# Splitting a 768-column product into 384 + 384 instead of 512 + 256

## Chip, cores and metric

The kernel runs on one core of one Trainium2 chip. The metric is device time in microseconds. The kernel before takes 2879.85 us, the median of three runs (2879.68 to 2881.93).

## What is computed

The reference is two layers of a diffusion backbone on 512 latent tokens and 256 context tokens of width 1024, in float32. Each layer is a SwiGLU feed-forward block, a token mixing block and a second feed-forward block, all of them modulated:

```
h   = modulate(rms_norm(x), shift, scale)
x  += 0.5 * gate * (silu(h @ w_gate) * (h @ w_up)) @ w_down        # width 2816
h   = modulate(rms_norm(x), shift, scale)
x  += gate * concat(attention(GQA), short_conv, attention(MLA)) @ w_out   # all from h @ w_in
x  += second half-step feed-forward, as the first
```

Latent and context tokens share all weights. Only the latent stream is returned, so the context stream ends after the attention of the second layer: three of the four feed-forward blocks work on all 768 tokens, the last one on the 512 latent tokens.

## The kernel before, in words

All activations are held transposed: the model dimension on the partitions (eight tiles of 128), tokens along the columns, latent tokens in columns 0 to 511 and context tokens in columns 512 to 767 of tiles that are 768 wide. A float32 product is made of three products of rounded parts: each operand is split into a high part and a remainder, and `mm3` (line 192) issues high times high, high times low and low times high. For each of the three it walks over `segs(cols)` (line 183), which cuts a column range at column 512: a product over all 768 tokens is thus one matmul of 512 columns and one of 256. Both read the same stationary weights, and each matmul instruction comes with a weight load of its own in the trace.

```
for st, mv, f, l in ((wh, rh, first, False), (wh, rl, False, False), (wl, rh, False, last)):
    for s in segs(cols):
        te.matmul(out=pt[:, s], lhsT=st, rhs=mv[:, s], start=f, stop=l)
```

`project` (line 197) calls `mm3` for every 128-row tile of the contraction: eight tiles, or seven or eight in the down projection. The result lies in a PSUM tile made by `ps()` (line 98), 1024 columns of float32, which are two banks of 512; there are two such tiles. Columns 0 to 511 of the product fill the first bank and columns 512 to 767 half of the second. Four more single banks come from `po()`.

In a feed-forward block (`ffn`, line 422) the 22 tiles of the inner width are done in three chunks of 8, 7 and 7. For each tile a gate and an up product are made into the two `ps` tiles; ScalarE takes silu out of the gate product, VectorE multiplies it with the up product, and the result is split again. The first two of the 22 tiles are done with latent and context columns apart, because their latent products are started while the norm ahead of them is still running. After each chunk `residual` (line 302) makes the down projection: eight output tiles over all columns, except that the last chunk of a block does only five in this way and the last three with latent and context columns apart. `update` (line 311) adds each product, times a per-row gate, to `xT`, in one VectorE instruction for the latent columns and one for the context columns.

Products over all 768 tokens are also made in `mixing` (line 625): the second convolution group (`conv`, line 645) in the first layer, the compressed keys (`ckv`) in both layers and the compressed queries (`cq`) in the first, with `evac` (line 779) and `Stats.square` (line 229) reading them, and five output tiles of the output projection of the first layer.

Weights come by DMA on the SP queue (`wload`, line 167, two buffers). ScalarE rounds them to the high part, VectorE subtracts to get the low part (`wsplit`, line 172, three buffers each). VectorE also computes the modulation vectors beside the feed-forward blocks (`mod_block`, line 128). Within a stretch marked by `chain(...)` and `unchain(...)` an engine keeps program order; elsewhere the framework's scheduler orders the instructions.

Of the kernel before, what the change touches and what calls it, by code (L numbers as in the profile page):

```python
# [15 lines left out]
P = 128  # L16
# [9 lines left out]
DEPTH = 2  # L26
EPS = 1e-6
LAT = slice(0, SEQ)
CTXS = slice(SEQ, T)
# [12 lines left out]
def tile_net(ctx: ExitStack, tc: tile.TileContext, a, out):  # L42
# [7 lines left out]
    class Engine:  # L50
        """An engine whose instructions keep the program order inside a chain and stay behind it."""

# [58 lines left out]

    # ---------------------------------------------------------------- constants
    ident = const.tile([P, P], F32, name="ident")
# [8 lines left out]

    # ---------------------------------------------------------------- modulation
    mod = {}
# [40 lines left out]

    # ---------------------------------------------------------------- weights
    def wload(src, w):
# [15 lines left out]
    def segs(cols):  # L183
# [6 lines left out]
        return r  # L190

    def mm3(pt, wh, wl, rh, rl, cols, first, last):
        for st, mv, f, l in ((wh, rh, first, False), (wh, rl, False, False), (wl, rh, False, last)):
            for s in segs(cols):
                te.matmul(out=pt[:, s], lhsT=st, rhs=mv[:, s], start=f, stop=l)

# [6 lines left out]

    # ---------------------------------------------------------------- rsqrt and norms
    def rsqrt_steps(ms, n, tag="rs", bufs=3):
        """1/sqrt(ms) of a [P, n] tile, and the steps that compute it."""
        hm, y, t = (small(n, tag=tag + c, bufs=bufs) for c in "abc")
        steps = [lambda: ve.tensor_scalar_mul(hm, ms, -0.5),
                 lambda: ve.tensor_scalar(out=y.bitcast(I32), in0=ms.bitcast(I32), scalar1=-0.5, scalar2=1597463007.0,
                                          op0=ALU.mult, op1=ALU.add)]  # L210
        for _ in range(3):
            steps += [lambda: ve.tensor_mul(t, y, y), lambda: ve.tensor_mul(t, t, hm),
                      lambda: ve.scalar_tensor_tensor(out=y, in0=t, scalar=1.5, in1=y, op0=ALU.add, op1=ALU.mult)]
        return y, steps
# [7 lines left out]
    class Stats:  # L222
        """sum over the model dim of x^2, one stream."""

# [3 lines left out]

        def square(self, x):
            self.sq = slot() if self.acc is None else temp()  # L230
            se.activation(out=self.sq[:, :self.w], in_=x[:, self.cols], func=AF.Square)

# [6 lines left out]

        def add(self, x):  # L240
            self.square(x)
            self.accumulate()
# [34 lines left out]
    class HMod:  # L277
        """hi and lo of (x*A)*R + B for one model tile and one stream"""

# [22 lines left out]
    def residual(blocks, rhs, gate, streams, nxt, pre=None, late={}):  # L302
        """x += gate * (W^T rhs) for streams of (columns, modulation row); nxt = (layer, mod index) of the norm that
        follows, or None. pre: weight sources of the first products after that norm. Returns h and (weights, products)."""
        g = mod[gate]
# [10 lines left out]
        for o in range(KD - ntail):  # L316
            pt = ps()
            project(pt, blocks(o), rhs, full)
            for n, (cols, i) in enumerate(streams):
                update(o, pt[:, cols], cols, i)  # L320
                if two:
                    S[n].add(xT[o])
# [13 lines left out]

        # the norm of the first stream runs beside the last products of the second
        s1 = []
# [81 lines left out]

    # ---------------------------------------------------------------- FFN
    def ffn(l, f, hin, streams, nxt, pre, npump, late={}):
# [7 lines left out]
        for ci, (m0, nm_) in enumerate(CHUNKS):  # L430
            acts = []
            for m in range(m0, m0 + nm_):
                wgu = [E[2 * m + j] if 2 * m + j < len(E) else wblock(a[("wg", "wu")[j]][i, m]) for j in range(2)]
                if 2 * m < len(E):
# [6 lines left out]
                    for j in range(2):  # L441
                        project(pts[j], wgu[j], h, c1)
                    parts = ((first[0][:, c0], first[1][:, c0], c0), (pts[0][:, c1], pts[1][:, c1], c1))
                else:
                    pts = [ps(), ps()]
                    for j in range(2):
                        project(pts[j], wgu[j], h, cols)
                    parts = ((pts[0][:, :w], pts[1][:, :w], cols),)
                sg = temp()
                for g, u, c in parts:  # L450
                    se.activation(out=sg[:, c], in_=g, func=AF.Silu)
                    ve.tensor_mul(sg[:, c], u, sg[:, c])
                ah, al = slot(F32R), slot(F32R)
# [18 lines left out]

    # ---------------------------------------------------------------- attention
    side = []

    def trickle(n=2):
        """small DVE steps of side work between the large ones"""
        for _ in range(n):
            if side:
                side.pop(0)()  # L480

    class Unit:
        """two query blocks of one head"""

# [27 lines left out]
        def transposes(self, g):  # L512
            """key tiles 2g, 2g+1 of P^T"""
            if g >= self.ng:
# [56 lines left out]
    def attend(units, jobs):  # L571
        """units as a pipeline, every engine in the order given here; jobs[n, place] holds the other work of step n."""
        chain("te")
# [45 lines left out]

    # ---------------------------------------------------------------- token mixing  # L620
    def wn_block(l, k, c0, w, eng=None):
# [3 lines left out]
    def mixing(l, hin, early, streams, nxt, pre):  # L625
# [4 lines left out]
        nqt = wq // P  # L630
        # per-layer vectors
        gq = cst("gqk", l, [P, 512])
# [9 lines left out]

        # ---- conv
        mix = [None] * 8
        def conv(c):
# [3 lines left out]
            def product(j):  # L649
                if c:  # L650
                    pt = ps()
                    project(pt, wbs[j], h, qcols)
                    return [pt[:, qcols]]
                r = [accs[j][:, LAT]]
# [7 lines left out]
            for src, cols in zip(product(0), parts):  # L662
                se.copy(u[:, cols], src)
            for src, cols in zip(product(1), parts):
                ve.tensor_mul(u[:, cols], src, u[:, cols])
            y = slot()
# [6 lines left out]
            for src, cols in zip(product(2), parts):  # L673
                ve.tensor_mul(y[:, cols], src, y[:, cols])
            mix[3 + c] = y

        # ---- q, k, kr, v token-major
        qk = [None] * NT
# [36 lines left out]

        # ---- q, k norm and rope (token-major)
        ms = pool.tile([P, NT, 9], F32, name=nm("st2"), tag="st2", bufs=1)
# [4 lines left out]
        def rope_a(y, sin, nh, dh, t2f, e1):  # L722
            """swap(y)*sin over a [P, nh, dh] view"""
            b = dh // 4
# [8 lines left out]
        def rope_b(y, t2, cos, nh, e0):  # L733
            """y = y*cos + t2"""
            e0.tensor_mul(y, y, bc(cos, 1, nh))
# [9 lines left out]
        def twice(t):  # L745
            """both key heads twice, for a transpose into both halves of the partitions"""
            x = qk[t]
# [20 lines left out]

        # ---- transposed projections: ckv, cq
        comp = {"ckv": [], "cq": []}  # L770
# [8 lines left out]
        def evac(pt, name, g, w):  # L779
            ch, cl = slot(F32R), slot(F32R)  # L780
            se.mul(ch[:, :w], pt[:, :w], g)
            ve.scalar_tensor_tensor(out=cl[:, :w], in0=pt[:, :w], scalar=g, in1=f32(ch)[:, :w], op0=ALU.mult, op1=ALU.subtract)
            comp[name].append((ch, cl))

        for i in range(5):
# [17 lines left out]
            if i < 4:  # L803
                evac(pt, name, g, w)
                stats[name].add(pt)

        # ---- transposed keys and queries of the GQA heads
        def colsT(c, n, t0, alloc):
# [37 lines left out]
        query_split(q0, 0)  # L846
        stats["cq"].square(pt)
        key_split(k1, slot(F32R), pool.tile([P, T], F32R, name=nm("k2"), tag="mscr", bufs=1))
        query_split(q0, 1)
        stats["cq"].accumulate()  # L850

        # ---- MLA up-projections (token-major)
        st3 = pool.tile([P, NT, 18], F32, name=nm("st3"), tag="st3", bufs=1)
# [32 lines left out]
        def heads_of(t):  # L886
            """views [P, heads, 96] of the keys of token tile t, with their heads; the last tile lies in spare columns"""
            if t == packed:
# [35 lines left out]

        # ---- MLA norms (token-major), as side work
        def factors(ts, c, parts, r, tag):
            """rsqrt(mean((r*x)^2) + eps) * r for the sums of squares in the columns c of st3"""
            n, w = ts.stop - ts.start, c.stop - c.start
# [48 lines left out]

        # ---- attention
        lat_units = ((0, 1), (2, 3))
# [34 lines left out]
        def mla_part(hd, which, t0):  # L1014
            """queries (0) or keys (1) of one head transposed, from token tile t0 on; split when complete"""
            tok, n, w = ((query_of, nqt, wq), (key_of, NT, T))[which]
# [99 lines left out]

        # ---- output projection
        mix_split(7)
# [6 lines left out]

    # ---------------------------------------------------------------- the network
    chain("te", "ve", "se")
# [257 lines left out]
```

## Time and profile before

| | |
|---|---|
| median of three runs | 2879.85 us (2879.68 to 2881.93) |
| span of the profiled execution | 2882.5 us |
| mean granted TensorE clock | 0.993 |
| TensorE (PE) busy | 2782.3 us, 97% of the span, 15824 matmuls |
| VectorE (DVE) busy | 1496.3 us, 52% |
| ScalarE (ACT) busy | 898.4 us, 31% |
| GpSimd (POOL) busy | 189.9 us, 7% |

All rows come from one profiled execution; its span is the time from its first to its last instruction, and no time is recorded for what lies outside it. Its span is 2.65 us above the median of the runs. PE is the matrix engine; PEld are its weight loads, which overlap the matmuls. Matmuls are pipelined: the duration of one contains its latency, so neighbouring matmuls overlap, and what a matmul costs in a dense stretch is the distance from its start to the start of the next (its pitch), which is a stretch's length over its count.

### The profile page before, as it was taken

The page shows a single profiled execution, that of the slowest core. Times are in us where ns is not written, and L with a number is a line of the kernel's source. Part 1 is how long each engine was busy: PE and PEld are TensorE (multiplying, and loading weights), DVE is VectorE, ACT ScalarE, POOL GpSimd, SP SyncE. Part 2 cuts the span into 40 slices and gives each one's busy share as a digit, 9 for nine tenths or more (in the row PEclk, how much of TensorE's full clock was granted, in tenths as well). Part 3 has the DMA queues.
Part 4 walks back from the last instruction along what each step waited for, and adds up shares of the span by engine and source line. Part 5 has one row for each costly group of instructions (what it writes and reads, how often), then busy time and mean ns, then how long its engine had stood idle before and what let it go on. Part 6 is the DMA issues. An engine that isn't in the chain of part 4 may idle for free.

```text
span 2882.5 us, 38311 instructions
## 1 busy us (share of the span) xinstructions
PE 2782.3 (97%) x15824; PEld 2407.2 (84%) x15824; DVE 1496.3 (52%) x2498; ACT 898.4 (31%) x1451; POOL 189.9 (7%) x225
## 2 busy tenths in 40 slices
PE   7999999999988999999999999999999989999999
PEld 4888888889778888888888888888887788888887
DVE  6763645263788667546343642222235798633333
ACT  4211212232467632112122321221223478422221
POOL 0000000011232210000000100000001233100000
PEclk9999999999999999999999999999999999999999
DMA  6542533212100125434232342212122100233332
GB/s 216 162 153 75 157 112 110 60 47 72 35 1 9 52 75 168 130 100 153 92 110 70 112 148 66 62 57 72 57 61 61 61 8 16 74 103 95 90 101 88
DMA packets 79167, 251.51 MB, mean 87 GB/s; under 512 B 10896, under 2 KB 16528, under 8 KB 78992
## 3 DMA queue, kind: packets, MB, share of 16 engines
q1 hardware_dynamic: 78992, 249.06, 27.7%
q8 instruction: 124, 2.03, 0.3%
q14 instruction: 51, 0.42, 0.0%
HBM read 246.93 MB, written 2.10 MB: 86 GB/s over the span
## 4 chain that ended last, share of the span: by engine, by line
PE 84%; DVE 8%; ACT 5%; issue 2%; DMA 1%; POOL 0%; SPq 0%; DVEq 0%; ACTq 0%; POOLq 0%
PE ps L60 74%; PE po L60 10%; DVE m L60 3%; DVE s L60 3%; ACT t L60 2%; ACT s L60 1%; ACT ph L60 1%; DVE t L60 1%; DMA wr<-in_wiN_dram 0%; DVE wl L60 0%; ACT wh L60 0%; ACT ot L60 0%; DVE kr L60 0%; DMA xT<-in_xT_dram 0%; DVE pl L60 0%
## 5 line engine op out<-in xcount | busy, mean ns | idle before, releaser
L60 PE MATMUL ps<-s,wh 128*128 128x512 f32 (+1 forms) x7794 | 1782.0, 342 | 4.1 <-ACT wh L60 3.8
L60 PEld LDWEIGHTS ps<-s,wh 128*128 128x128 f32 x7794 | 1233.8, 188 | 197.5 <-ACT wh L60 4.5
L60 PE MATMUL ps<-s,wl 128*128 128x512 f32 (+1 forms) x3897 | 1086.9, 343 | 0.8 <-DVE wl L60 0.8
L60 ACT CAST wh<-wr 128x1024 fp32r<-128x1024 f32 (+1 forms) x308 | 314.8, 1024 | 1486.9 <-PE ps L60 984.6
L60 PEld LDWEIGHTS ps<-s,wl 128*128 128x128 f32 x3897 | 624.4, 188 | 96.4 <-DVE wl L60 1.9
L60 DVE TENSOR_TENSOR wl<-wr,wh 128x1024 fp32r<-128x1024 f32 (+3 forms) x298 | 354.2, 1190 | 269.1 <-ACT wh L60 267.0
L60 DVE SCALAR_TENSOR_TENSOR xT<-ps,mod,xT 128x256 f32<-128x256 f32 (+1 forms) x209 | 110.6, 566 | 407.7 <-PE ps L60 407.7
L60 DVE SCALAR_TENSOR_TENSOR mscr<-mr,sb 128x1024 f32<-128x1024 f32 x224 | 273.8, 1222 | 61.3 <-DMA mr<-in_wm_dram 57.8
L60 DVE TENSOR_TENSOR t<-ps,t 128x768 f32<-128x768 f32 (+2 forms) x91 | 76.7, 843 | 423.9 <-PE ps L60 422.9
L60 PE MATMUL po<-s,s 128*128 128x256 f32 (+2 forms) x856 | 133.9, 312 | 10.0 <-DVE s L60 3.1
L60 PE MATMUL po<-s,wh 128*128 128x512 f32 (+1 forms) x478 | 139.2, 375 | 0.7 <-ACT s L60 0.4
L60 PEld LDWEIGHTS po<-s,s 128*128 128x128 f32 x856 | 124.9, 194 | 14.4 <-DVE s L60 4.0
L238 POOL TENSOR_TENSOR s<-s,t 128x256 f32<-128x256 f32 x15 | 13.1, 876 | 1822.0 <-ACT t L60 1820.4
L60 DVE TENSOR_REDUCE m<-ps 128x1 f32<-128x768 f32 (+2 forms) x126 | 103.5, 821 | 27.7 <-PE ps L60 27.2
L60 PE MATMUL po<-ident,t 128*128 128x128 f32 x684 | 101.0, 279 | 15.0 <-ACT t L60 14.0
L60 ACT ACTIVATE t<-ps,m 128x768 f32<-128x768 f32 (+1 forms) x120 | 99.0, 825 | 23.0 <-DVE m L60 22.3
L60 PEld LDWEIGHTS po<-s,wh 128*128 128x128 f32 x478 | 86.4, 190 | 18.7 <-issue 0.9
L60 PEld LDWEIGHTS po<-ident,t 128*128 128x128 f32 x684 | 79.7, 143 | 19.7 <-ACT t L60 18.2
L60 PE MATMUL po<-s,wl 128*128 128x512 f32 (+1 forms) x239 | 90.1, 377 | 1.5 <-POOL wl L177 1.5
L60 ACT ACTIVATE t<-ps 128x768 f32<-128x768 f32 (+4 forms) x116 | 80.3, 692 | 18.1 <-DVE s L60 18.1
L60 DVE TENSOR_TENSOR s<-po,s 128x256 fp32r<-128x256 f32 (+5 forms) x139 | 71.5, 541 | 14.5 <-ACT s L60 12.2
L60 DVE TENSOR_TENSOR s<-t,s 128x768 fp32r<-128x768 f32 (+1 forms) x88 | 77.7, 883 | 0.9 <-ACT s L60 0.9
(147 smaller groups left out, 1964.5 us busy)
## 6 DMA issues: line engine op xcount, KB each, us to landing
mr<-in_wm_dram SPq DMA_DIRECT2D x128, 512.0 KB, 3.6
wr<-in_wg_dram SPq DMA_DIRECT2D x88, 512.0 KB, 3.5
wr<-in_wu_dram SPq DMA_DIRECT2D x88, 512.0 KB, 3.5
wr<-in_wd_dram SPq DMA_DIRECT2D x64, 448.0 KB, 3.4
wr<-in_wd_dram SPq DMA_DIRECT2D x32, 512.0 KB, 3.6
wr<-in_wiT_dram SPq DMA_DIRECT2D x22, 512.0 KB, 3.5
wr<-in_wo_dram SPq DMA_DIRECT2D x14, 512.0 KB, 3.5
s<-in_wm_dram SPq DMA_DIRECT2D x16, 384.0 KB, 6.5
```

Source lines behind the costliest of these rows:

```text
L60: f(*args, **kw)
L238: (eng or ve).tensor_add(self.acc[:, :self.w], self.acc[:, :self.w], sq[:, :self.w])
```

## The change

A product over all 768 columns is cut at column 384 instead of column 512. The first 384 columns go to columns 0 to 383 of the `ps` tile (first bank), the other 384 to columns 512 to 895 (second bank). Everything that reads such a product reads two pieces of 384 columns a bank apart, and writes them to 768 neighbouring columns. Products over the latent or the context columns alone are left as they are. Docstrings and comments are removed too.

```diff
+HALF = T // 2
+BANK = 512
...
+    def halves_of(cols):
+        if cols.start == 0 and cols.stop == T:
+            return [(slice(0, HALF), slice(0, HALF)), (slice(HALF, T), slice(BANK, BANK + HALF))]
+        return [(s, s) for s in segs(cols)]
+    def banks(pt):
+        return pt.rearrange("p (a b) -> p a b", b=BANK)[:, :, 0:HALF]
+    def pairs(t):
+        return t[:, 0:T].rearrange("p (a b) -> p a b", b=HALF)
...
+    def of_ps(pt, cols):
+        return banks(pt) if whole(cols) else pt[:, cols]
+    def of_sb(t, cols):
+        return pairs(t) if whole(cols) else t[:, cols]
     def mm3(pt, wh, wl, rh, rl, cols, first, last):
         for st, mv, f, l in ((wh, rh, first, False), (wh, rl, False, False), (wl, rh, False, last)):
-            for s in segs(cols):
-                te.matmul(out=pt[:, s], lhsT=st, rhs=mv[:, s], start=f, stop=l)
+            for s, d in halves_of(cols):
+                te.matmul(out=pt[:, d], lhsT=st, rhs=mv[:, s], start=f, stop=l)
...
             for n, (cols, i) in enumerate(streams):
-                update(o, pt[:, cols], cols, i)
+                if full.stop < T:
+                    update(o, pt[:, cols], cols, i)
+                else:
+                    for s, d in halves_of(full):
+                        lo, hi = max(s.start, cols.start), min(s.stop, cols.stop)
+                        if lo < hi:
+                            update(o, pt[:, d.start + lo - s.start:d.start + hi - s.start], slice(lo, hi), i)
...
-                    parts = ((pts[0][:, :w], pts[1][:, :w], cols),)
+                    parts = ((of_ps(pts[0], cols), of_ps(pts[1], cols), lambda t: of_sb(t, cols)),)
                 sg = temp()
-                for g, u, c in parts:
-                    se.activation(out=sg[:, c], in_=g, func=AF.Silu)
-                    ve.tensor_mul(sg[:, c], u, sg[:, c])
+                for g, u, of in parts:
+                    se.activation(out=of(sg), in_=g, func=AF.Silu)
+                    ve.tensor_mul(of(sg), u, of(sg))
```

In `residual` the latent columns 0 to 511 now lie in both banks, so `update` is called three times for an output tile instead of two: for 384 and 128 latent columns and for 256 context columns. `conv`, `evac` and `Stats.square` get the same two-piece views.

## Rows read from the trace of the kernel before

**Rows 1.** The profile page, its first part: busy time, share of the span and instructions of each engine.
```profile
PE 2782.3 (97%) x15824; PEld 2407.2 (84%) x15824; DVE 1496.3 (52%) x2498; ACT 898.4 (31%) x1451; POOL 189.9 (7%) x225
```

**Rows 2.** The span in stretches: from and to (us), length, then busy time and instructions of PE, PEld, DVE, ACT and POOL, the granted clock, the DMA share and GB/s. The second, sixth and eighth stretch below lie inside the three feed-forward blocks on 768 columns, the last one in the block on 512.
```profile
0.00:77.00 77.00, 58.34 (x285) 36.42 (x286) 47.81 (x109) 34.74 (x61) 0.70 (x6) 0.96 0.60 202
77.00:589.00 512.00, 512.00 (x2948) 448.31 (x2949) 267.89 (x390) 104.67 (x120) 0.00 (x0) 1.00 0.38 119
589.00:720.00 131.00, 125.16 (x739) 112.08 (x738) 65.64 (x134) 36.96 (x71) 18.01 (x14) 1.00 0.19 58
720.00:974.00 254.00, 221.53 (x1519) 201.58 (x1518) 204.34 (x403) 174.55 (x379) 72.00 (x92) 0.98 0.05 17
974.00:1077.00 103.00, 99.70 (x554) 85.20 (x553) 60.82 (x109) 33.91 (x52) 7.60 (x5) 1.00 0.23 72
1077.00:1580.00 503.00, 503.00 (x2887) 439.37 (x2887) 247.10 (x361) 100.42 (x113) 0.00 (x0) 1.00 0.38 118
1580.00:1637.00 57.00, 53.30 (x287) 44.64 (x286) 42.30 (x82) 20.60 (x33) 7.58 (x5) 1.00 0.23 74
1637.00:2141.00 504.00, 504.00 (x2897) 440.46 (x2896) 156.26 (x193) 100.35 (x113) 0.00 (x0) 1.00 0.27 82
...
2525.00:2882.00 357.00, 352.37 (x1532) 284.11 (x1530) 122.21 (x154) 86.75 (x105) 0.00 (x0) 1.00 0.31 95
```

**Rows 3.** Groups of PE's matmuls, shapes kept apart: names, contraction by stationary columns, moving shape, count, busy us, mean ns of one, idle us ahead of them. A matmul into `ps` from `s` (activations) and `wh` or `wl` (weights) is one of `project`'s.
```profile
L60 PE MATMUL ps<-s,wh 128*128 128x512 f32 x4258 | 1514.9, 394 | 3.8 <-ACT wh L60 3.8
L60 PE MATMUL ps<-s,wh 128*128 128x256 f32 x3536 | 946.8, 280 | 0.3 <-ACT sb L60 0.3
L60 PE MATMUL ps<-s,wl 128*128 128x512 f32 x2129 | 840.8, 395 | 0.8 <-DVE wl L60 0.8
L60 PE MATMUL ps<-s,wl 128*128 128x256 f32 x1768 | 494.6, 280 | 0.0
```

**Rows 4.** Pieces of the chain of work that ended last: start us, length us (start of the piece to start of the next), what, and how many instructions. The first two lie in the output projection of the first layer (768 columns as 512 + 256 alternating, then 512 alone), the last two in that of the second (512 alone, then 256 alone). `ps` is written in both of its banks only in the first.
```profile
974.32 42.00 PE ps L60 x240
1016.32 16.80 PE po L60 x72
...
2450.92 28.00 PE ps L60 x120
2478.92 8.64 PE po L60 x72
```

**Rows 5.** The timeline of PE in the product of queries by token tile (moving operand 384 columns wide, the weights `wn` at columns 0 and 384 of one 768-column tile): start us, us to the end of the last, what, how many; and then the first matmuls of a 384-column product after 256-column ones.
```profile
653.80 17.15 PE L60 MATMUL po<-s,s 128*128 128x384 f32 x98
...
862.16 0.34 PE L60 MATMUL ps<-wh,s 128*128 128x384 f32 x1
862.34 0.34 PE L60 MATMUL ps<-wl,s 128*128 128x384 f32 x1
862.52 0.51 PE L60 MATMUL ps<-wh,s 128*128 128x384 f32 x2
862.87 0.34 PE L60 MATMUL ps<-wl,s 128*128 128x384 f32 x1
863.04 0.51 PE L60 MATMUL ps<-wh,s 128*128 128x384 f32 x2
```

**Rows 6.** Groups of VectorE's instructions, shapes kept apart: the updates of `xT` out of a `ps` tile; columns as in rows 3.
```profile
L60 DVE SCALAR_TENSOR_TENSOR xT<-ps,mod,xT 128x256 f32<-128x256 f32 x141 | 65.0, 478 | 92.0 <-PE ps L60 92.0
L60 DVE SCALAR_TENSOR_TENSOR xT<-ps,mod,xT 128x512 f32<-128x512 f32 x68 | 51.0, 751 | 315.7 <-PE ps L60 315.7
```

**Rows 7.** The timeline of VectorE in the down projection of the first feed-forward block: start us, us, what, and in brackets its idle time ahead of it and who ended that.
```profile
241.37 1.14 DVE L60 SCALAR_TENSOR_TENSOR xT<-ps,mod,xT 128x512 f32<-128x512 f32 x2 [6.12 <-PE ps L60]
242.43 1.22 DVE L60 TENSOR_TENSOR wl<-wr,wh 128x1024 fp32r<-128x1024 f32 x1
249.77 1.14 DVE L60 SCALAR_TENSOR_TENSOR xT<-ps,mod,xT 128x512 f32<-128x512 f32 x2 [6.12 <-PE ps L60]
```

**Rows 8.** Groups of ScalarE's reads of a `ps` tile, shapes kept apart. The 576-column one (`uq`) reads two pieces of 288 columns a bank apart; the other two read neighbouring columns.
```profile
L60 ACT ACTIVATE t<-ps 128x768 f32<-128x768 f32 x64 | 51.6, 806 | 13.0 <-DVE s L60 13.0
L60 ACT ACTIVATE t<-ps 128x512 f32<-128x512 f32 x22 | 13.1, 594 | 5.1 <-DVE s L60 5.1
L60 ACT ACTIVATE t<-ps 128x576 f32<-128x576 f32 x10 | 6.6, 659 | 0.0
```

**Rows 9.** PE's weight loads in a stretch of the output projection of the first layer where products over 768 columns follow each other (974.4 to 1016 us): count, busy us, mean ns of one, idle us.
```profile
L60 PEld LDWEIGHTS ps<-s,wh 128*128 128x128 f32 x158 | 24.1, 187 | 3.5
L60 PEld LDWEIGHTS ps<-s,wl 128*128 128x128 f32 x80 | 12.2, 187 | 1.8
```

More of the change, by code (lines that the diff above doesn't have):

```diff
@@ L190, in segs, with whole @@
         return r
+    def halves_of(cols):
[6 more added lines that the diff above has]
+        return t[:, 0:T].rearrange("p (a b) -> p a b", b=HALF)
+    def whole(cols):
+        return cols.start == 0 and cols.stop == T
+    def of_ps(pt, cols):
+        return banks(pt) if whole(cols) else pt[:, cols]
+    def of_sb(t, cols):
+        return pairs(t) if whole(cols) else t[:, cols]
     def mm3(pt, wh, wl, rh, rl, cols, first, last):
         for st, mv, f, l in ((wh, rh, first, False), (wh, rl, False, False), (wl, rh, False, last)):
-            for s in segs(cols):
-                te.matmul(out=pt[:, s], lhsT=st, rhs=mv[:, s], start=f, stop=l)
+            for s, d in halves_of(cols):
+                te.matmul(out=pt[:, d], lhsT=st, rhs=mv[:, s], start=f, stop=l)
     def project(pt, wb, rhs, cols):
@@ L227, in __init__, with square @@
             self.w = cols.stop - cols.start
-        def square(self, x):
+        def square(self, x, wide=False):
             self.sq = slot() if self.acc is None else temp()
-            se.activation(out=self.sq[:, :self.w], in_=x[:, self.cols], func=AF.Square)
+            if wide:
+                se.activation(out=pairs(self.sq), in_=banks(x), func=AF.Square)
+            else:
+                se.activation(out=self.sq[:, :self.w], in_=x[:, self.cols], func=AF.Square)
         def accumulate(self, sq=None, eng=None):
@@ L238, in accumulate, with add @@
                 (eng or ve).tensor_add(self.acc[:, :self.w], self.acc[:, :self.w], sq[:, :self.w])
-        def add(self, x):
-            self.square(x)
+        def add(self, x, wide=False):
+            self.square(x, wide)
             self.accumulate()
@@ L319, in residual @@
             for n, (cols, i) in enumerate(streams):
-                update(o, pt[:, cols], cols, i)
+                if full.stop < T:
+                    update(o, pt[:, cols], cols, i)
+                else:
+                    for s, d in halves_of(full):
+                        lo, hi = max(s.start, cols.start), min(s.stop, cols.stop)
+                        if lo < hi:
+                            update(o, pt[:, d.start + lo - s.start:d.start + hi - s.start], slice(lo, hi), i)
                 if two:
@@ L442, in ffn @@
                         project(pts[j], wgu[j], h, c1)
-                    parts = ((first[0][:, c0], first[1][:, c0], c0), (pts[0][:, c1], pts[1][:, c1], c1))
+                    parts = ((first[0][:, c0], first[1][:, c0], lambda t: t[:, c0]),
+                             (pts[0][:, c1], pts[1][:, c1], lambda t: t[:, c1]))
                 else:
@@ L652, in product @@
                     project(pt, wbs[j], h, qcols)
-                    return [pt[:, qcols]]
+                    return [of_ps(pt, qcols)]
                 r = [accs[j][:, LAT]]
@@ L662, in conv @@
             for src, cols in zip(product(0), parts):
-                se.copy(u[:, cols], src)
+                se.copy(of_sb(u, cols), src)
             for src, cols in zip(product(1), parts):
-                ve.tensor_mul(u[:, cols], src, u[:, cols])
+                ve.tensor_mul(of_sb(u, cols), src, of_sb(u, cols))
             y = slot()
@@ L673, in conv @@
             for src, cols in zip(product(2), parts):
-                ve.tensor_mul(y[:, cols], src, y[:, cols])
+                ve.tensor_mul(of_sb(y, cols), src, of_sb(y, cols))
             mix[3 + c] = y
@@ L780, in evac @@
             ch, cl = slot(F32R), slot(F32R)
-            se.mul(ch[:, :w], pt[:, :w], g)
-            ve.scalar_tensor_tensor(out=cl[:, :w], in0=pt[:, :w], scalar=g, in1=f32(ch)[:, :w], op0=ALU.mult, op1=ALU.subtract)
+            src, hi, lo = of_ps(pt, slice(0, w)), of_sb(ch, slice(0, w)), of_sb(cl, slice(0, w))
+            se.mul(hi, src, g)
+            ve.scalar_tensor_tensor(out=lo, in0=src, scalar=g, in1=f32(hi), op0=ALU.mult, op1=ALU.subtract)
             comp[name].append((ch, cl))
@@ L804, in mixing @@
                 evac(pt, name, g, w)
-                stats[name].add(pt)
+                stats[name].add(pt, w == T)
         def colsT(c, n, t0, alloc):
@@ L846, in mixing @@
         query_split(q0, 0)
-        stats["cq"].square(pt)
+        stats["cq"].square(pt, w == T)
         key_split(k1, slot(F32R), pool.tile([P, T], F32R, name=nm("k2"), tag="mscr", bufs=1))
```

## The prediction

> **What bounds the kernel now.** I began with the busy shares [rows 1]: PE is busy for 2782.3 of 2882.5 us, the next engine for 52%. A share of 97% does not say that PE is at its best, only that it is rarely idle, so the next view is the span in stretches [rows 2]. Inside the three feed-forward blocks on 768 columns PE is busy for 512.00 of 512.00, 503.00 of 503.00 and 504.00 of 504.00 us at a granted clock of 1.00, which is 2.4 GHz. Nothing waits there; time goes only where matmuls become cheaper. Outside, in the attention (720 to 974 us), PE is busy for 221.53 of 254 us and VectorE for 204.34: that part waits on other things and the change hardly touches it.
>
> Next, how many matmuls does the change reach [rows 3]? Products of 256 columns into `ps` from `s` and `wh` or `wl` are 3536 + 1768 = 5304. From the code, 669 of them belong to products over context columns or a half of the latent ones alone (the first two inner tiles of each block, the last three output tiles, the first convolution group, the second layer's halves). That leaves **4635 pairs** of 512 + 256. I also summed them directly: a 768-column block has 20 inner tiles x 2 products x 24, and 8 x 24 + 8 x 21 + 5 x 21 in the down projections, 1425 pairs; three blocks have 4275. `mixing` has 72 in the convolution, 96 for `ckv` in both layers, 72 for `cq` and 120 in the first layer's output projection, 360 together. 4275 + 360 = 4635, the same.
>
> **The price of a pair.** The mean duration in [rows 3] (394 and 280 ns) contains latency and is no price. The pitch comes from dense pieces of the chain [rows 4]. The 768-column stream takes 42.00 us for 240 matmuls, 350.0 ns a pair, of which 768 columns at 2.4 GHz are 320.0. Alone, 512 columns take 16.80 us / 72 = 233.33 ns (and 28.00 / 120 = 233.33), 20.0 above their columns; 256 columns take 8.64 / 72 = 120.0, 13.3 above.
>
> The kernel before also has 384-column matmuls, with the moving operand at columns 0 and 384 of one 768-column tile, just as the change reads it [rows 5]. 98 of them take 17.15 us from first start to last end; less the latency of the last (0.34 us, same group) that is 16.81 us over 97 starts, **173.3 ns**, 13.3 above the 160.0 of its columns. So the 512-column form is the one with the larger overhead (20.0 against 13.3), and a pair of 384s should take 2 x 173.3 = 346.7 ns: **3.33 ns less per pair**.
>
> What no row shows is 384 columns with the destination changing bank at every matmul. I bound it from both sides. Below: the alternating stream of 512 + 256 is 3.33 ns cheaper than its parts alone (350.0 against 353.3), so alternation may itself be worth up to 3.33 ns a pair, and a 384 pair could take 343.3. Above: the first 384-column matmuls after a 256-column product start 180 ns apart before settling at about 173 [rows 5], and a pair could pay that each time, 360. I take 346.7, by the row nearest in shape and in moving operand.
>
> **The change part by part.**
>
> *Matmuls.* 4635 x 3.33 ns = **15.4 us less**. Of the pairs, 4275 + 120 lie in the stretches where PE has nothing to wait for, 14.7 us. The other 240 (0.8 us) lie near 589 to 720 us and its counterpart in the second layer, where PE is idle for 6 us of 131 [rows 2]; some of theirs may be lost, too little to matter. Instruction counts on PE stay the same: two matmuls and two weight loads per pair.
>
> *The third update.* 68 VectorE updates of 512 columns become 68 of 384 and 68 of 128. The line through 256 columns (478 ns) and 512 (751 ns) [rows 6] has 1.07 ns a column and 205 ns fixed, so 384 costs about 614 and 128 about 341: 205 ns more per output tile, 13.9 us over all, as estimates. I cost this at nothing. What hides it is seen in the down projection [rows 7]: an output tile takes 8.40 us of PE, VectorE does its updates and one weight split in it and then sits idle for 6.12 us until PE ends the next. Queued behind the third update is that split's `wl`, for a product that comes two tiles later. Without this cover the price would be the whole 13.9 us and would eat the gain.
>
> *Two-piece reads.* The silu, the multiplications, `evac`, the squares and the convolution read two pieces a bank apart. Such a read exists: 576 columns in two pieces take 659 ns, where the line through 512 (594) and 768 (806) gives 647 for neighbouring columns [rows 8]. At most 12 ns more, on engines 20 to 52% busy in the blocks [rows 2]; 64 silus and as many products would be under 2 us, hidden. VectorE's two-piece cost has no row here; I bound it by the same 12 ns and by nothing below. Bank dependencies do not change: the result was in two banks before as well.
>
> *Weight loads.* Each matmul keeps its own load. They take 187 ns each and follow each other in pairs every 350 ns with idle time left, 3.5 + 1.8 us in 41.6 [rows 9]; in the 384-column chain a load per 173 ns already keeps pace [rows 5]. The pair now gives both loads an equal cover, so nothing becomes late here.
>
> *DMA and queues.* No transfer is added or moved. Weights are asked for 1% sooner at most, at a DMA share of 0.27 to 0.38 in the blocks [rows 2].
>
> **Sum.** 2882.5 us of span less 15.4 is 2867.1. The profiled span stands 2.65 us above the median of the runs, 2879.85, so the forecast is **2864.4 us**, 0.54% less.
>
> **A rule that speaks against it.** In [rows 4] the overhead of the pair is 30.0 ns over two matmuls, 15.0 each if it is taken as equal. The Trainium skill (TensorE: Matmul & The Clock Gate, section Back-to-back issue gap) gives the gap between matmuls at full clock as columns over 2.4 GHz plus a constant 2.5 ns; by that a pair of any split is an estimated 325 ns and the change is worth nothing. The trace disagrees on both halves so far: the overhead is 20.0 ns at 512 columns and 13.3 at 384 and 256 [rows 4, 5], neither small nor constant.
>
> **The rivals.**
>
> *The overhead belongs to the number of matmuls, not to their width* (no change). Then 15.0 ns a matmul stays in the mixed stream whatever the split, the pair stays at 350.0, and the time stays at 2879.9 us. For it: the mixed stream is cheaper than the sum of its parts, so prices of chains do not simply add. Against it: the 384-column chain, at 13.3. Chance 0.13.
>
> *Alternating banks is worth 3.33 ns in itself.* Then the new pair gains it too, 343.3 ns: 6.67 ns x 4635 = 30.9 us less, 2849.0 us. For it: 350.0 against 353.3. Against it: 256 and 384 alone both carry 13.3 ns and only 512 alone carries 20.0 [rows 4, 5], so it is as well explained by an extra of the 512-column form of which a 256 beside it hides half; then 384s have nothing left to gain. Chance 0.14.
>
> *A change of bank costs the start of a chain* (slower). At 180 ns for each matmul [rows 5] the pair takes 360 ns, 10 ns x 4635 = 46.4 us more, 2926.2 us. It decides as soon as the 384-column pitch exceeds 175.0 ns, at every one of the pairs. For it: the three first starts at 180. Against it: the present stream changes bank at every matmul at 350.0, below its parts. With it I count a smaller loss of the same sign, the scheduler placing instructions outside the chained stretches differently, so that a weight split ends late. Chance 0.07.
>
> *The change does not reach the pairs*, a cut that stays at 512 in some of the callers: the sum of pairs from the code and from the rows agree, and every one goes through `mm3`. I give it no chance of its own.
>
> **How the numbers follow.** The forecast at 346.7 has 0.66. A measurement of this kernel can tell about 0.2% from no change, 5.76 us or 1.24 ns a pair: the pair must come below 348.8 ns. Faster is the forecast and the bank rival, 0.80; the same is 0.13, slower 0.07. The range leaves out these last two, 0.20 together: it reaches down to 2849, the bank rival, and up to 2876, where a pair saves only 0.8 ns (or a quarter of the gain is left after waits elsewhere).
>
> **What the profile after would show.** Right: `ps` matmuls of 384 columns, 9270 of them less a few missing records, and of `xT` updates 68 each of 384 and 128; a dense piece of the output projection's chain at 346.7 ns a pair where it was 350.0; the stretches of 1425 pairs each shorter by 4.75 us with PE still busy throughout; the attention and the last block, on 512 columns, as long as before. Wrong: a pair at 350 or above in a dense piece (the rule or the bank-change rival), or the pair at 346.7 and PE idle inside a block with `wl`, `xT` or the silu as the releaser, which would be the third update or the two-piece reads coming through.

## The result, and the profile after

The changed kernel takes 2891.26 us (median of 5 runs, 2886.82 to 2893.18) against 2881.21 us for the kernel before (5 runs): a ratio of 1.0035, 95% interval 1.0023 to 1.0047. That is slower by 10 us where 15 us less was forecast, outside the range of 2849 to 2876.

The matmuls of 384 columns into `ps`, which answer to [rows 3], 9270 together:

```profile
L62 PE MATMUL ps<-s,wh 128*128 128x384 f32 x6180 | 1343.3, 339 | 0.7 <-ACT wh L62 0.7
L62 PE MATMUL ps<-s,wl 128*128 128x384 f32 x3090 | 797.2, 339 | 0.3 <-DVE wl L62 0.3
```

The dense pieces of the chain of work that ended last, in the changed kernel (start us, length us, what, how many matmuls), which answer to [rows 4]:

```profile
74.90 515.28 PE ps L62 x2946
970.80 42.40 PE ps L62 x240
1013.20 16.81 PE po L62 x72
1074.12 507.94 PE ps L62 x2887
1638.67 509.26 PE ps L62 x2898
2529.02 352.02 PE ps L62 x1528
```

The same pieces before that [rows 4] does not hold:

```profile
76.87 512.01 PE ps L60 x2946
1077.22 503.19 PE ps L60 x2887
1637.00 504.51 PE ps L60 x2898
2525.36 352.02 PE ps L60 x1528
```

A pair of 384s costs 42.40 us / 120 = **353.3 ns**, where 512 + 256 cost 350.0 and 346.7 was forecast. The second and third block are longer by 4.75 us each, which is 1425 pairs x 3.33 ns to the digit. The first block has as many pairs, at the same two prices by the starts in the trace, but its piece grew by 3.27 us only: in the profiled execution of before it begins while the granted clock is 0.77 (mean of 74 to 80 us, so in part at the lower level), in that of after at 1.00. Products of 512 columns alone are unchanged (the last block, 352.02 us both times; 16.81 / 72 = 233.5 ns). The stretches (length, then busy time of PE, PEld, DVE, ACT, POOL, as in [rows 2]) show that PE waits for nothing in them:

```profile
1074.10:1582.06 507.96, 507.96 (x2889) 507.96 (x2888) 249.68 (x381) 100.69 (x114) 0.00 (x0) 1.00 0.37 116
1638.70:2147.90 509.20, 509.20 (x2899) 509.20 (x2898) 159.31 (x213) 100.63 (x114) 0.00 (x0) 1.00 0.26 81
```

So what the blocks lose is all in the pitch of the matmuls, the distance from one start to the next. What is new beside it is the weight loads' column: 507.96 us busy in 507.96, where before it was 439.37 in 503.00 [rows 2]. That is not a bound by itself: a load is recorded as 187 to 188 ns in every kernel here, so at any pitch below that the records overlap and read as busy throughout. The faster versions below read the same.

VectorE did as forecast. Its groups that answer to [rows 6], and its timeline that answers to [rows 7]:

```profile
L62 DVE SCALAR_TENSOR_TENSOR xT<-ps,mod,xT 128x256 f32<-128x256 f32 x141 | 64.9, 477 | 92.5 <-PE ps L62 92.5
L62 DVE SCALAR_TENSOR_TENSOR xT<-ps,mod,xT 128x384 f32<-128x384 f32 x68 | 42.0, 618 | 312.4 <-PE ps L62 312.4
L62 DVE SCALAR_TENSOR_TENSOR xT<-ps,mod,xT 128x128 f32<-128x128 f32 x68 | 23.3, 342 | 0.0
```

```profile
247.84 1.27 DVE L62 SCALAR_TENSOR_TENSOR xT<-ps,mod,xT 128x384 f32<-128x384 f32 x3 [6.08 <-PE ps L62]
249.03 1.22 DVE L62 TENSOR_TENSOR wl<-wr,wh 128x1024 fp32r<-128x1024 f32 x1
```

618 and 342 ns where 614 and 341 were estimated; three updates, one weight split, then 6.08 us of idle time until PE ends the next output tile (6.12 before).

4635 pairs x 3.33 ns are 15.4 us, and the medians differ by 10. The remaining 5 us are not explained. In the two profiled executions the dense pieces run 13 us longer after the change and the spans only 2.5 us, so the rest is shorter by 10.7 us: 2.0 ahead of the first block, 4.8 between it and the first output projection, 2.8 between the third block and the last, 1.2 at the end. The granted clock differs there from one execution to the other (0.94 before and 0.97 after in the first 60 us, 0.98 and 0.99 from 720 to 960 us). That this makes the difference is not shown.

### The profile page after: what moved, and what is told of

It reads as the page before. It is cut to its first block, busy times and chain, and to the rows that moved or that the text cites. A ratio compares the mean times of both kernels' runs of the same rounds, so it can differ in the third digit from the quotient of the medians.

```text
span 2885.0 us, 38390 instructions
## 1 busy us (share of the span) xinstructions
PE 2789.7 (97%) x15824; PEld 2623.2 (91%) x15824; DVE 1504.6 (52%) x2566; ACT 897.5 (31%) x1451; POOL 189.1 (7%) x225
## 4 chain that ended last, share of the span: by engine, by line
PE 85%; DVE 9%; ACT 5%; issue 1%; DMA 1%; SPq 0%; POOL 0%; DVEq 0%; ACTq 0%
PE ps L62 74%; PE po L62 10%; DVE m L62 3%; DVE s L62 3%; ACT t L62 2%; ACT s L62 1%; DVE t L62 1%; ACT ph L62 0%; ACT wh L62 0%; DVE wl L62 0%; DMA wr<-in_wiN_dram 0%; DVE kr L62 0%; ACT ot L62 0%; DMA s<-in_wm_dram 0%; DVE pl L62 0%
## 5 line engine op out<-in xcount | busy, mean ns | idle before, releaser
L62 PE MATMUL ps<-s,wh 128*128 128x384 f32 (+2 forms) x7794 | 1792.7, 344 | 3.8 <-ACT wh L62 3.5
L62 PEld LDWEIGHTS ps<-s,wh 128*128 128x128 f32 x7794 | 1395.4, 188 | 59.8 <-ACT wh L62 4.2
L62 PE MATMUL ps<-s,wl 128*128 128x384 f32 (+2 forms) x3897 | 1093.8, 345 | 0.8 <-DVE wl L62 0.8
L62 PEld LDWEIGHTS ps<-s,wl 128*128 128x128 f32 x3897 | 712.7, 188 | 27.1 <-DVE wl L62 1.9
L62 DVE SCALAR_TENSOR_TENSOR xT<-ps,mod,xT 128x256 f32<-128x256 f32 (+2 forms) x277 | 119.3, 479 | 404.8 <-PE ps L62 404.8
```

The source lines that it names most:

```text
L62: f(*args, **kw)
```

## The experiments

**Is it the change of bank, the moving offset, or the weights loaded twice?** Three edits of the changed kernel and one of the kernel before.

```diff
# a_384_by_bank: one bank after the other
+        for s, d in halves_of(cols):
+            for k in range(n):   # ... the three products of tile k into pt[:, d]
# b_512_by_bank: the same in the kernel before, over segs(cols)
# c_one_bank: both matmuls of a pair into one bank
+                d = slice(0, HALF) if k < n // 2 else slice(BANK, BANK + HALF)
+                    for j in range(2):   # ... rhs=mv[:, j * HALF:(j + 1) * HALF], out=pt[:, d]
# d_same_columns
-                te.matmul(out=pt[:, d], lhsT=st, rhs=mv[:, s], ...
+                te.matmul(out=pt[:, d], lhsT=st, rhs=mv[:, 0:HALF] if whole(cols) else mv[:, s], ...
```

> The changed kernel, but a product over 768 columns issues all its matmuls into the first bank (columns 0 to 383) and then all into the second (columns 384 to 767), so the destination changes bank once per product instead of at every matmul; the computation is the whole one. The changed kernel showed 353.3 ns a pair. If the change of bank at every matmul is what costs (theory 1), the pair is 346.7 ns in a dense stretch and the time is 4635 x 3.33 = 15.4 us below the kernel before, near 2866. If it is the moving operand that starts at column 384 (theory 2), the sum of the two stays at 353.3 ns and the time near the changed kernel's 2891. If it is the weights loaded twice in a row (theory 3), the pair falls too, since here the same weights follow each other for two of three matmuls only; 348 to 351 ns.

> The kernel before with the same regrouping: all 512-column matmuls of a product, then all its 256-column ones. If alternating 512 and 256 columns is worth 3.33 ns a pair over the two alone, as the rows of before suggest, the pair is 353.3 ns and the time about 15 us above the kernel before, 2896. If the price of a pair does not hang on the order, it stays at 350.0 and 2881.

> The changed kernel with both matmuls of a pair writing the same bank: the first half of the contraction accumulates into the first bank, the rest into the second, so the sums mix the two halves of the tokens and the output is not the reference's. Moving operand still alternates between columns 0 and 384, weights still come twice in a row, only the bank no longer alternates. Theory 1 (bank): 346.7 ns a pair. Theories 2 (moving offset) and 3 (weights twice): 353.3.

> The changed kernel with both matmuls of a pair reading columns 0 to 383 of the moving tile, so the second half of the tokens gets the first half's products and the output is not the reference's. The bank still alternates, weights still come twice in a row, only the moving offset is gone. Theory 1 (bank): 353.3 ns a pair. Theory 2 (moving offset): 346.7. Theory 3 (weights twice): 353.3.

The 240-matmul piece of the output projection in the four, a, b, c and d in this order:

```profile
972.41 42.40 PE ps L62 x240
```
```profile
976.28 42.40 PE ps L60 x240
```
```profile
972.88 42.40 PE ps L62 x240
```
```profile
974.33 42.40 PE ps L62 x240
```

All are at 353.3 ns a pair. a and c rule out the changing bank, d rules out the moving offset, and a speaks against the weights loaded twice, which should have been 348 to 351 ns there. a took 2889.80 us, a ratio of 1.0037 (1.0023 to 1.0051). All three theories fell. b came out as expected (2896.38 us, one run): 512 and 256 in separate runs cost the sum of what they cost alone, so alternating them is worth 3.33 ns a pair in this kernel.

**Which operand?** The query product at 173.33 ns a matmul differs from a gate product in where both operands lie and in what they hold.

```diff
# e_sources, var = inner tile modulo 6
+            sh, sl = (rh[:, 0:P], rl[:, 0:P]) if var in (1, 3) else (wh[:, 0:P], wh[:, 0:P]) if var == 4 else (wh[:, c], wl[:, c])
+            mh, ml = (wh, wl) if var in (2, 3) else (rhs[0][0], rhs[0][0]) if var == 5 else (rh, rl)
```

> The changed kernel with the operands of the gate and up products of a block exchanged in turn over the inner tiles (the output is not the reference's): as it is; stationary operand out of an activation tile; moving operand out of a weight tile; both; one stationary operand for the whole product; one moving tile for the whole product. Regrouping by bank, one bank for a pair, and one column range for both halves each left a 384-column matmul of these products at 176.67 ns, where the query product of before has 173.33 with activations stationary and weights moving. If the source of the stationary operand matters, the second and fourth form fall to 173.3; if that of the moving operand does, the third and fourth; if it is the change of stationary or of moving tile between neighbours, the fifth or the sixth. If none falls, the price belongs to the place in the stream and not to the operands.

Matmuls inside one inner tile (names are output, then operands, `s` an activation tile, `wh` and `wl` weight tiles; count, busy us, mean ns of one, idle us): weights moving over weights; activations over activations; one weight tile stationary under moving activations:

```profile
L62 PE MATMUL ps<-wh,wl 128*128 128x384 f32 x14 | 3.6, 334 | 0.0
L62 PE MATMUL ps<-wh 128*128 128x384 f32 x14 | 3.6, 334 | 0.0
...
L62 PE MATMUL ps<-s,s 128*128 128x384 f32 x28 | 6.1, 334 | 0.0
...
L62 PE MATMUL ps<-s,wh 128*128 128x384 f32 x41 | 7.4, 339 | 0.0
```

Where both operands come from the same pool of tiles (the tiles that share their buffers) a matmul takes 334 ns from start to end, and the starts in the trace are 173.33 ns apart; stationary weights with moving activations take 339 and 176.67, as in the changed kernel. One stationary operand or one moving tile for a whole product changed nothing (176.67). Neither operand's source decides alone: it is the combination. Activations stationary under moving weights have two prices: 173.4 in three of the four inner tiles that had them, 176.7 in the fourth, in every block. The order of the products tells them apart: the three follow products of weights over weights at 173.3 to 173.4, the fourth follows a down projection at 176.6 to 176.7. In all twelve such tiles the pitch is that of the stream just ahead; that this is the cause was not tested.

**Does the cut have an optimum?** Each inner tile cut elsewhere.

```diff
+CUTS = (512, 496, 480, 448, 416, 400, 384, 368, 352, 320, 288, 256)
...
+                        CUT[0] = CUTS[m % len(CUTS)]
```

> The changed kernel with the gate and up products cut at another column for each inner tile, from 512 + 256 by way of 384 + 384 to 256 + 512, each piece evacuated by its own instructions; the computation is the whole one. If a fixed overhead per matmul held, all cuts would cost the same. If price is proportional to columns with a rounding up per matmul, some cut costs 350.0 ns or a little less and others up to some 357, with no slope over the cut. If the 512-column form carries an extra of its own, every cut without it is below 350; 384 + 384 at 353.3 already speaks against that. Best guess: 348 to 358, the lowest at 512 + 256 or 256 + 512.

From the starts in the trace, ns a pair by the width of the first piece: 512: 350.0; 496: 353.0; 480: 353.3; 448: 353.4; 416: 354.3; 400: 351.2; 384: 353.3; 368: 353.1; 352: 353.3; 320: 353.4; 288: 353.3; 256: 350.9. As expected there is no slope, and 512 + 256 is the best cut. Nine of the twelve cuts, 384 + 384 among them, cost 353.0 to 354.3: what is special is 512 + 256, not 384 + 384. A cut that is no multiple of 64 columns also shifts where the second piece begins within 256 bytes, so the seven such cuts (496, 480, 416, 400, 368, 352, 288) are not a test of the cut alone.

**Does the place of the weights matter?** The tiles' start addresses in the built program say where pools lie: activation tiles (`s`) start 224 bytes above a multiple of 256, `wh` and `wl` 128 above one. The halves, the 128-column slices of the weights and the buffers are multiples of 256 or 512 bytes apart, so this holds for every pair of the kernels before and after.

```diff
# g_offsets
-            hi = pool.tile([P, 1024], F32R, ...)
+            hi = pool.tile([P, 1024 + 32], F32R, ...)[:, OFF[0]:OFF[0] + 1024]      # lo alike
+                OFF[0] = 8 * (m % 5)      # 0, 32, 64, 96, 128 bytes
```

> The exchange of operands gave 173.33 ns wherever stationary and moving operand came from the same pool of tiles (activations with activations, weights with weights), and 176.67 with stationary weights and moving activations. In the built program the activation tiles begin 32 bytes above a multiple of 64 and the weight tiles at a multiple of 64. Here the split weights lie 0, 32, 64, 96 or 128 bytes into a slightly wider tile, in turn over the inner tiles (inner tile number modulo 5), and the three blocks on 768 columns use the cuts 384 + 384, 512 + 256 and 448 + 320; the computation is the whole one. If the relative place of the two operands matters (theory 4), the pitch changes with the offset, and where both are 32 above a multiple of 64 (32 and 96 bytes) the 384 pair is 346.7 ns and perhaps the 512 + 256 pair below 350.0 too. If the tiles' places do not matter, all offsets give 353.3, 350.0 and 353.4 ns a pair.

The wider tiles made neighbouring buffers differ by 128 bytes modulo 256, so each product has a place for its high parts and another for its low parts. ns a 384 pair, by the places of the high and low parts above a multiple of 256 (starts in the trace, addresses in the program; the median over 2 to 65 products each): 0 and 128: 351.2; 128 and 0: 353.2; 32 and 160: 350.0; **160 and 32: 346.8**; 64 and 192: 349.2; 192 and 64: 350.5; 96 and 224: 350.9; 224 and 96: 348.7. For 512 + 256: 348.8 to 352.1, for 448 + 320: 348.7 to 351.1. The place of the split weights matters: it is what the edit changes from one inner tile to the next in one execution, and the changed kernel, with one place for all, has 353.3 in each. It does so in steps of 32 bytes and with 32 and 160 unlike 160 and 32, so not by the multiple of 64 that I had guessed.

**The change in another place.** One unused tile ahead of the weight tiles, nothing else. By the addresses in the built programs it shifts all tiles that are allocated behind it, the raw weights and VectorE's scratch tiles too, and leaves `xT` and the activation tiles where they were. That the split weights are what counts among the shifted tiles rests on g_offsets.

```diff
# after_pad32, before_pad32; 24 columns in ..._pad96, 40 in ..._pad160
+    pe.memset(pool.tile([P, 8], F32, name="pad", tag="pad", bufs=1), 0.0)
     Rs = pool.tile([P, D], F32, name="Rs", tag="mscr", bufs=1)
```

> The changed kernel with one unused tile of 32 bytes a partition ahead of the weight tiles (and its memset on GpSimd): all split weights then begin 160 bytes above a multiple of 256, the activation tiles 224 as before; nothing else is changed. In the kernel with offsets, a 384 pair took 346.67 ns with the high parts at 160 and the low parts at 32 above a multiple of 256, and 350.0 the other way round; two to one, that is 343.3 ns for all at 160 and 353.3 for all at 32. Theory 4 (relative place of stationary and moving operand): 343.3 ns a pair, 4635 x 6.67 = 31 us below the kernel before, a ratio near 0.989. If the place of the weights matters only with a mixture of offsets, the pair stays at 353.3 and the ratio at 1.0035.

> The kernel before (512 + 256) with the same 32-byte tile ahead of the weights. In the kernel with offsets the 512 + 256 pair took 348.9 ns with the high parts at 160, 351.9 with them at 32: 346 for all at 160 by the same two to one. Theory 4: 346 (345 to 348) ns a pair, 4635 x 4 = 19 us below the kernel before, a ratio near 0.994; the 384 cut is then the better one by some 12 us in this place of the weights and the worse one in the old place. If places do not matter: 350.0 and a ratio of 1.000.

> The changed kernel with 96 bytes ahead of the weights, which puts them at 224 above a multiple of 256, the same as the activations. That is the relative place of the query product of before, where one 384-column matmul takes 173.33 ns. Theory 4: 346.7 ns a pair, about 15 us below the kernel before. If only the absolute place of the weights counts, no value is foreseen.

> The changed kernel with 160 bytes ahead of the weights, which puts them at 32 above a multiple of 256, 64 beyond the activations. Theory 4, by the two-to-one working from the offsets: 353.3 ns a pair, as the changed kernel, so about 12 to 15 us above the kernel before: a control that an unused tile alone brings nothing.

> The kernel before (512 + 256) with 96 unused bytes ahead of the weights, the partner of after_pad96. If 512 + 256 is favoured by the old place alone, the pair is at 353.3 ns as it is with 32 bytes and the products of 512 alone near 227 ns: 4635 x 3.33 = 15 us more and some 1500 to 2400 x 6 ns = 9 to 14 us less, so near the kernel before, ratio 1.000 to 1.003. If every place other than with 32 bytes is as good for it as the old one, 350.0 or less and a ratio near 0.996.

> The changed kernel with 96 bytes ahead of the weights once more, timed: by its one time before (2846.8), a ratio of 0.988 to 0.990 to the kernel before; 384 pairs at 346.7 ns and products of 512 alone at 227 ns.

> The kernel before with 160 unused bytes ahead of the weights, the partner of after_pad160 (2862.2, where the 384 pair is 346.7 ns in most products and the products of 512 alone are at 233.3). If 512 + 256 is favoured by the old place alone, 353.3 ns a pair and about 2894; if not, 350.0 or less and at most 2880.

Pieces of the chain in after_pad32, before_pad32, after_pad96_timed, before_pad96 and after_pad160:

```profile
964.65 41.60 PE ps L62 x240
1006.25 16.48 PE po L62 x72
1066.49 498.36 PE ps L62 x2887
2499.43 345.33 PE ps L62 x1528
```
```profile
972.45 42.40 PE ps L60 x240
1014.85 16.48 PE po L60 x72
1074.99 507.69 PE ps L60 x2887
2483.72 8.16 PE po L60 x72
2527.68 345.13 PE ps L60 x1528
```
```profile
960.63 41.62 PE ps L62 x240
1002.25 16.36 PE po L62 x72
1062.41 498.44 PE ps L62 x2887
2495.41 342.12 PE ps L62 x1528
```
```profile
977.16 42.40 PE ps L60 x240
1019.56 16.38 PE po L60 x72
1079.75 507.94 PE ps L60 x2887
2531.99 342.12 PE ps L60 x1528
```
```profile
963.61 41.60 PE ps L62 x240
1065.82 502.16 PE ps L62 x2887
1624.43 499.65 PE ps L62 x2898
```

| weights start, above a multiple of 256 | 384 pair, ns | 512 + 256 pair, ns | 512 alone, ns | time with 384 | time with 512 + 256 |
|---|---|---|---|---|---|
| 128 (as it was) | 353.3 | 350.0 | 233.3 | 2891.26, ratio 1.0035 | 2881.21 |
| 160 (32 bytes) | 346.7 | 353.3 | 228.9 | 2849.49, ratio 0.9894 (0.9880 to 0.9907) | 2880.23, ratio 1.0002 (0.9993 to 1.0011) |
| 224 (96 bytes) | 346.7 | 353.3 | 227.2 | **2844.84, ratio 0.9881 (0.9867 to 0.9895)** | 2878.35, ratio 0.9998 (0.9989 to 1.0007) |
| 32 (160 bytes) | 346.7, in the second block 349.3 | 353.3 | 233.3 | 2862.18 (one run) | 2890.22 (one run) |

Ratios are to the kernel before on the same chip, from 4 to 11 runs each; after_pad96 had 2846.80 in one run, after_pad96_timed is the same kernel. Pairs are the 240-matmul piece over 120, confirmed by the starts in most products of each trace; 512 alone is the `po` piece over 72.

Theory 4 holds so far as the place of the weights counts: a shift by 32 bytes changes the pitch of nearly all these products. That it is the place relative to the activations is not shown. Its working by two to one failed: 343.3 ns was expected at 160 and 346 for 512 + 256 there, 353.3 for 384 at 32; measured were 346.7, 353.3 and 346.7. I know of no formula that gives the price from the place. before_pad32 was expected at 0.994 and is at 1.0002, since its dearer pair (353.3) eats what its cheaper products of 512 alone give (the last block, 345.13 us against 352.02). As expected if 512 + 256 was favoured by its old place alone, before_pad96 and before_pad160 have 353.3 as well.

The place does not settle everything. In after_pad160 every product of the second block has 349.3 ns a pair and every one of the third 346.7, with weights in the same three buffers, and in before_pad96 5 of the 198 products over 768 columns have 346.5 to 346.7 ns where the others have 353.5. So do the products in e_sources under moving weights: the same places, modulo 256 bytes, allow more than one pitch.

## Why the prediction was wrong

*The number of pairs* (4635) was right: 6180 + 3090 matmuls of 384 columns stand in the trace, 9270. *That PE is all that bounds the blocks* was right, and so was *the cover* over the third update and the two-piece reads: the second and third block grew by exactly their pairs' pitch.

*The step that failed is the price of a pair*, "2 x 173.3 = 346.7 ns", taken "by the row nearest in shape and in moving operand" [rows 5]. The query product has the same shape and the same column offsets, but its weights lie in the activations' pool; both of its operands start 224 bytes above a multiple of 256. The change's products have weights at 128 under activations at 224. In that place 384 columns cost 176.67 ns. With both at 224 (after_pad96) they cost exactly the forecast 173.33, and so do they at 160. So the pair was priced 6.7 ns too low, 346.7 against the 353.3 measured: 30.9 us over 4635 pairs, which turns 15.4 us of gain into 15.4 us of loss. With 32 or 96 bytes of padding in both kernels the 384 cut does gain, 6.7 ns a pair or 30.9 us by the pitch, and the ratios differ by 0.9894 - 1.0002 = -0.0108 and 0.9881 - 0.9998 = -0.0117, 31 and 34 us.

*The reason given*, an extra of the 512-column form, was a misreading too. Each form's overhead depends on the place: 512 alone has 20.0, 15.6 and 13.9 ns above its columns in three places.

*The rivals.* The bank rival for the slow side has the right sign, and its mechanism is refuted by c_one_bank and its 46 us by the 10 us measured. Its 180 ns came from starts that are rounded to 10 ns: from 862.16 to 863.04 us lie five matmuls [rows 5], 176 ns each on average. Alternating banks as a gain is refuted by the same run, since the pair does not care about the bank. That 512 + 256 is cheaper than the sum of its parts, for which the prediction considered the bank, is a property of the old place: with 32 bytes of padding 353.3 ns is not below 228.9 + 113.3 = 342.2 (8.16 us / 72 = 113.3 for 256 alone there; other products of 256 alone in that run have 117.8, which makes 346.7). The rival of a constant overhead per matmul is refuted as well: one and the same instruction stream has 33.3 ns a pair at 128 and 26.7 at 160 or 224.

The formula that the prediction quotes from the Trainium skill (TensorE: Matmul & The Clock Gate, section Back-to-back issue gap) is given there for an isolated matmul, not for a stream with a weight load per matmul. No run has its 325 ns a pair, the lowest products are at 346.5, and what a matmul takes above its columns is no constant here: 13.9 to 20.0 ns for 512.

The Trainium skill (TensorE: Matmul & The Clock Gate, section Step-by-step: what each phase is for) says that the streaming operand and the weight load have independent read ports, so that loading the next weights does not take read bandwidth from the running matmul. If that were all that sets the time, moving the weights should change nothing; in g_offsets the place of the split weights alone moves a pair between 346.8 and 353.2 ns, and from the changed kernel to after_pad32 it goes from 353.3 to 346.7. The measurement decides. It does not say whether the two reads disturb each other: which port, buffer or row inside the memory makes the pitch hang on the place no run here shows.

## What to carry to other kernels

A pitch read from another product of the same trace is a price only for operands that lie alike: compare where the tiles start before borrowing it. When a stream of matmuls is the bound and its pitch stands above its columns, try the place of the weight tiles in steps of 32 bytes early; one unused tile costs a line. And judge a cut or a reordering in more than one place: here the same edit is 0.35% slower in one place and over 1% faster than the kernel before in two others.

## What the runs showed that was not expected

The pitch of identical matmuls hangs on the start address of the weight tiles: 173.33 or 176.67 ns for 384 columns, 227.2, 228.9 or 233.3 ns for 512, 350.0 or 353.3 for 512 + 256, all at a granted clock of 1.00. Whether the absolute place or the place relative to the moving operand counts is not separated: same-pool operands were at 173.33 ns both at 224 (activations) and at 128 (weights), which speaks for the relative one, but 160 and 32 give 173.33 too under activations at 224. Nor is the place alone enough: activations under moving weights in e_sources take 173.4 or 176.7, always that of the stream ahead of them, and the second block of after_pad160 has 349.3 ns where the third has 346.7. Whether and what one product hands to the next was not tested. A version that beats both kernels came of it, after_pad96_timed, at 2844.84 us.
